# Encoder layer on one core: pooling's and the attention's projections as pairs, the middle's stages in another order, tiles kept in DRAM between their making and their use

## The chip, the cores and the metric

The kernel runs on one core of one Trainium2 chip, as one program and one launch. The metric is the device time of that core in microseconds; the time before is 2240.25 us, the median of three runs (2239.61 to 2243.97). A core has five engines, each with its own queue of instructions that it takes in order: TensorE (PE in the profile) multiplies, VectorE (DVE) and ScalarE (ACT) do elementwise work, GpSimd (POOL) and SyncE (SP) here only issue DMAs. Work on two engines overlaps unless one waits for the other's result, or for a place in memory.

## The reference

One layer of a bidirectional encoder over 256 tokens of width 2048, in float32:

```
x = x + 0.5 * swiglu(rmsnorm(x, ffn1_norm), ffn1_w_gate, ffn1_w_up, ffn1_w_down)
h = rmsnorm(x, mix_norm)
proj = h @ w_in       # u_pool 1024 | q 1536 | k 1536 | v 1536 | q_mem 1024 | gates 3 x 2048
y_pool = pooling_branch(u_pool, pool_w, pool_scale) @ w_up_pool
y_attn = dilated_attention_branch(q, k, v, positions) @ w_up_attn      # 3 groups of 4 heads, rotary q and k
y_mem  = memory_branch(q_mem, rmsnorm(mem, mem_norm), w_mem_kv) @ w_up_mem      # 4 heads, 256 memory tokens
merged = gates_0 * y_pool + gates_1 * y_attn + gates_2 * y_mem
x = x + merged @ w_out
x = x + 0.5 * swiglu(rmsnorm(x, ffn2_norm), ffn2_w_gate, ffn2_w_up, ffn2_w_down)
return rmsnorm(x, final_norm)
```

## The kernel before

**Products.** Every float32 factor is split into a high part (float32r, made by ACT, `wh`) and the rest (made by DVE, `wl`), and a product is three matmuls: low times high, high times high, high times low. A step of PE is one such matmul, 128x128 times 128x512. A plain product of the 256 tokens with 512 columns of a weight (`gemm`) takes, for 2048 rows of the weight, 16 row blocks x 2 token halves x 3 = 96 matmuls into two PSUM banks called `acc`. Its weights come as four tiles `wf` of 128x2048 (1 MB each), loaded by SP; each needs one `wh` on ACT and one `wl` on DVE.

**Pairs.** `pair_gemm` makes two such products at once, 1024 columns, in eight steps over pairs of row blocks, into eight banks called `q1` to `q8`. A step with eight products costs 24 matmuls, as much as in two plain products. A step out of the tuple `sevens` takes seven products, 21 matmuls, by a scheme of sums of blocks; it costs DVE more: `sums` of weight blocks (one add of 128x1024, two of 128x512), their split (`sumsh` on ACT in two pieces, `sumsl` on DVE), and a split of three blocks instead of four (128x1536). The left operand must have sums too; `lhs_mix` has them for steps 0, 2, 3 and 5 (`SEVEN_MIX`). When a bank's last product is done, `finish` brings it to SBUF, with four subtractions and four additions on DVE and one copy on ACT where sevens are used.

**The middle.** Between the two SwiGLU blocks stand, in this order: keys, values and query of the memory branch, twice (`mem_head` makes the four heads beside them); two plain products for pooling (u, with `pooling` beside what follows); for each of three head groups g the plain products Q, K, V, and, ahead of groups 1 and 2, the pooling gates of two chunks as a pair (`gated_pair(0, 0)`, `gated_pair(0, 2)`) with their two products with `w_up_pool`; the memory gates 0 and 1 as plain products with the attention's scores beside them (`attend`); the memory gates 2 and 3 as a pair; the attention gates as two pairs with three sevens each; four products with `w_out`. `PAIRED` says which gates are pairs and with which sevens.

After Q or K, `rotate` turns the columns by the rotary tables on DVE, and `turn_pieces` transposes the result: two DVE transposes of 32x32 squares into a spare tile, then 16 ACT copies of 32x256 (`qkT<-swap`).

**Places.** Large tiles share a ring of 23 slots. Held for long before are `lhs_mix` (6 slots), the memory's and pooling's left operands (`mem_lhs`, `pool_lhs`, 2 each), one `qkT` for each head group, and two tiles for the three V and the mask (`v01`, `v2`). One step of a pair with sevens uses 6 slots while it runs (`wf`, `wh`, `wl`, `sums`, `sumsh`, `sumsl`). Four tiles `tmp` and two `half` serve the rest.

**What sets the order.** The source only records instructions (`Plan.record`); `Plan.issue` then plays them through with costs of its own, gives out places, and writes each engine's order. Pieces of side work stand in a list (`later`, filled by `queue`) and are taken out between the row blocks of a product (`pop`). DMAs of SP and of POOL go out in the order of recording. All instructions have the line of the call in `Plan.issue`, L240, so the profile is read by tile names.

Of the kernel before, what the change touches and what calls it, by code (L numbers as in the profile page):

```python
# [9 lines left out]
F32 = mybir.dt.float32  # L10
# [417 lines left out]
def tile_encoder_layer(ctx: ExitStack, tc: tile.TileContext, a: dict, out: bass.AP):  # L428
# [816 lines left out]


    w_in = a["w_in"]
    mem_lhs = [lslot() for _ in range(2)]
    THREE = ((1, 0), (0, 0), (0, 1))

    def mem_head(qT, kT, v, h, L):
# [53 lines left out]
        return [scores], [*turns, parts], [lambda: values(0), lambda: values(1), lambda L=L: result(L)]  # L1305

    rope_work = rope_pieces()
    for n in range(2):
        queue(rope_work.pop(0))
        acc = gemm(mem_lhs_in, a["w_mem_kv"], 0, n * CW)  # L1310
        s = tmp([P, T, CW], "km")
        scaled_copy(s, acc, mem_rstd[0])
        kT = transposed(s)
        acc = gemm(mem_lhs_in, a["w_mem_kv"], 0, MEMW + n * CW)
        v = slot([P, 2, T, CW], F32R, "vm")
        scaled_split(v, acc, mem_rstd[0])
        queue(rope_work.pop(0))
        acc = gemm(lhs_mix, w_in, 0, C_M + n * CW)
        s = tmp([P, T, CW], "qm")
        scaled_copy(s, acc, rstd2)  # L1320
        qT = transposed(s)
        pending.add(id(mem_lhs[n]))
        (s0, t0, v0), (s1, t1, v1) = [mem_head(qT, kT, v, h, mem_lhs[n]) for h in range(2)]
# [4 lines left out]
        queue(lambda n=n: pending.discard(id(mem_lhs[n])))  # L1328


    band = slot([P, 4, T, S], F32R, "band")
# [51 lines left out]
    for n in range(2):  # L1383
        pending.add(id(pool_lhs[n]))
        queue(rope_work.pop(0))
        acc = gemm(lhs_mix, w_in, 0, n * CW)
        u = slot([P, 2, T, CW], F32R, "u")
        scaled_split(u, acc, rstd2)
        queue(lambda n=n, u=u: pooling(n, u))
        queue(lambda n=n: pending.discard(id(pool_lhs[n])))  # L1390


    MD = [dr.tile([P, T, CW], F32, name=f"merged{n}") for n in range(NCH)]
# [81 lines left out]
    qkT = [slot([P, 2, HEADS, S], F32, "qkT") for _ in GROUPS]  # L1475
    v01 = slot([P, 2, T, CW], F32, "v01")
    v2 = slot([P, 2, T, CW], F32, "v2")
    values = [v01[:, 0], v01[:, 1], v2[:, 0]]
    mask = v2[:, 1]
    nc.gpsimd.dma_start(out=mask, in_=a["mask"])  # L1480

    for g in range(3):
        if g:
            all_gated(0, (2 * g - 2, 2 * g - 1), pool_lhs, a["w_up_pool"])
        for sel, c0 in enumerate((C_Q, C_K)):
            acc = gemm(lhs_mix, w_in, 0, c0 + g * CW)
            r = tmp([P, T, CW], "rot")
            s = tmp([P, T, CW], "swap")

            def rotate(t, acc=acc, r=r, s=s):  # L1490
                src = acc[t].rearrange("p (h d) -> p h d", h=HEADS)
# [3 lines left out]
                nc.vector.tensor_mul(rt, src, cos.unsqueeze(1).to_broadcast([P, HEADS, P]))  # L1495
# [3 lines left out]
                nc.vector.tensor_mul(  # L1499
                    st[:, :, H:], src[:, :, :H], sin[:, H:].unsqueeze(1).to_broadcast([P, HEADS, H])  # L1500
                )
                nc.vector.tensor_add(r[:, t], r[:, t], s[:, t])

            queue(*(lambda t=t, f=rotate: f(t) for t in range(T)), soon=True)
            queue(*turn_pieces(qkT[g][:, sel], r, s))
        acc = gemm(lhs_mix, w_in, 0, C_V + g * CW)
        scaled_copy(values[g], acc, rstd2)

    attn_lhs = [lslot()]

# [1 line left out]
    def scores(h, state):  # L1512
        p = tmp([P, T, 2 * S], "p")
        for t in range(T):
            b = bank([P, 2 * S])
            blk = slice(t * P, (t + 1) * P)
            nc.tensor.matmul(b[:, :S], qkT[0][:, 0, h, blk], qkT[0][:, 1, h], start=True, stop=True)
            for g in (1, 2):
                c = S + (g - 1) * P
                nc.tensor.matmul(  # L1520
                    b[:, c : c + P], qkT[g][:, 0, h, blk], qkT[g][:, 1, h, blk], start=True, stop=True
                )
            nc.vector.tensor_add(p[:, t], b, mask[:, t])
# [12 lines left out]

    def turned_scores(state):
        def piece(i):
            if i == 0:
                state["pT"] = blocks_of(state["p"])  # L1540
                state["turns"] = turn_pieces(state["pT"], state["p"], tmp([P, T, 2 * S], "squares"))
            state["turns"][i]()

        return [lambda i=i: piece(i) for i in range(6)]
# [17 lines left out]
    def attend(n):  # L1562

        mine = [heads.pop(0) for _ in range(HEADS // len(alone))]
        states = [{} for _ in mine]
        for h, state in zip(mine, states):
            queue(lambda h=h, state=state: scores(h, state))
            queue(*[lambda: None] * (5 // len(mine)))
# [13 lines left out]
    all_gated(  # L1582
        1, range(NCH), attn_lhs, a["w_up_attn"], done=lambda n: merged_lhs.append(transposed(merged[n], shift=MERGED_MOVED))
    )


    lhs3 = pair_tiles(SEVEN)
# [150 lines left out]
```

## Time and profile before

| | |
|---|---|
| Runs | 2239.61, 2243.97, 2240.25 us; median 2240.25 |
| Profiled execution | 2241.2 us, of which 2239.5 us from the first to the last instruction |
| Granted TensorE clock | 0.998 of full speed |
| VectorE, ScalarE busy | 1892.4 us (85%), 1630.1 us (73%) |
| POOL | 264 instructions, 199.8 us |
| DMA | 531.36 MB, 237 GB/s on the mean |

The page cuts the span in 40 slices; the middle lies in slices 13 to 28 (696 to 1551 us). There DVE is busy 5 to 9 tenths and ACT 4 to 7, while in most slices of the two SwiGLU blocks DVE stands at 9 tenths or more. The profile calls PE busy throughout; since the end of a matmul is modelled, the rate is read from the distance of starts, that is, from the length of an unbroken run of matmuls divided by their count.

### The profile page before, as it was taken

Reading aid. Unit: us, or ns where it says so; the run is one execution under the profiler, and the core shown is the slowest. Engines: PE = TensorE matmul, PEld = TensorE weight load, DVE = VectorE, ACT = ScalarE, POOL = GpSimd, SP = SyncE. Lnnn points to the kernel's source line nnn. Section 1 sums busy time; section 2 is a strip of 40 time slices with the busy share of each in tenths; the row PEclk is TensorE's granted clock in tenths of the full one; section 3 lists DMA queues with packets and bytes.
Section 4 is the critical chain, followed back from the end, with each engine's and each line's share of the span. In section 5 each row is a group of like instructions: output and inputs, shape, how many; then the busy total and the mean of one; then the engine's idle time right before and its main releaser. Section 6 shows DMA issues by size and latency. Waiting matters only on the chain.

```text
span 2239.5 us, 26840 instructions
## 1 busy us (share of the span) xinstructions
PE 2223.7 (99%) x9906; PEld 1838.4 (82%) x9906; DVE 1892.4 (85%) x1738; ACT 1630.1 (73%) x2101; POOL 199.8 (9%) x264
## 2 busy tenths in 40 slices
PE   9999999999999999999999999999999999999998
PEld 7888888888887888888788888878888888888887
DVE  7999999999986865785776688977999999999995
ACT  8877777877777687654546774779777777777773
POOL 0011111111120000000000000000011111111110
PEclk9999999999999999999999999999999999999999
DMA  9688898988995564565464577666589989888892
GB/s 376 213 249 248 257 273 259 258 251 259 274 320 202 185 229 151 179 223 217 169 256 172 176 241 266 253 211 212 186 226 264 255 249 270 254 250 254 260 340 105
DMA packets 128995, 531.36 MB, mean 237 GB/s; under 512 B 15072, under 2 KB 15328, under 8 KB 102752
## 3 DMA queue, kind: packets, MB, share of 16 engines
q1 hardware_dynamic: 94608, 444.15, 55.7%
q0 software_dynamic: 33824, 84.95, 18.6%
q8 instruction: 77, 1.26, 0.2%
q10 hardware_dynamic: 432, 0.56, 0.1%
q14 instruction: 54, 0.44, 0.1%
HBM read 460.40 MB, written 50.33 MB: 228 GB/s over the span
## 4 chain that ended last, share of the span: by engine, by line
PE 95%; DMA 1%; DVE 1%; issue 1%; ACT 1%; POOL 0%; SPq 0%; DVEq 0%; POOLq 0%; ACTq 0%
PE q L240 48%; PE acc L240 29%; PE down L240 18%; PE bank L240 2%; DVE wl L240 1%; DMA wf<-in_ffn_w_up 1%; DMA xt<-in_memT 1%; ACT wh L240 0%; DMA wf<-in_w_in 0%; DVE up L240 0%; SPq L240 0%; POOL xs L240 0%; DVE squares L240 0%; POOL x L240 0%; DVE xs L240 0%
## 5 line engine op out<-in xcount | busy, mean ns | idle before, releaser
L240 DVE TENSOR_TENSOR wl<-wf,wh 128x2048 fp32r<-128x2048 f32 (+2 forms) x422 | 876.2, 2085 | 114.6 <-ACT wh L240 112.7
L240 ACT ACTIVATE wh<-wf 128x2048 fp32r<-128x2048 f32 (+2 forms) x422 | 732.1, 1750 | 127.2 <-DMA wf<-in_w_in 68.1
L240 PE MATMUL acc<-wh,lhs 128*128 128x512 f32 x1568 | 485.7, 391 | 0.0
L240 PE MATMUL down<-wh,lhs 128*128 128x512 f32 x1152 | 356.4, 391 | 0.0
L240 ACT ACTIVATE sumsh<-sums 128x1024 fp32r<-128x1024 f32 x266 | 280.9, 1060 | 98.0 <-DVE sums L240 95.8
L240 PE MATMUL q<-wh,seven 128*128 128x512 f32 x1102 | 342.9, 389 | 0.0
L240 PEld LDWEIGHTS acc<-wh,lhs 128*128 128x128 f32 x1568 | 293.4, 188 | 60.1
L240 DVE TENSOR_TENSOR sumsl<-sums,sumsh 128x2048 fp32r<-128x2048 f32 x133 | 303.5, 2282 | 46.1 <-ACT sumsh L240 43.9
L240 PE MATMUL q<-sumsh,seven 128*128 128x512 f32 x1064 | 321.3, 389 | 0.0
L240 PE MATMUL q<-wh,lhs 128*128 128x512 f32 x1024 | 310.4, 390 | 2.1 <-ACT wh L240 2.1
L240 PE MATMUL acc<-wl,lhs 128*128 128x512 f32 x784 | 305.7, 390 | 1.6 <-DVE wl L240 1.6
L240 PEld LDWEIGHTS down<-wh,lhs 128*128 128x128 f32 x1152 | 215.1, 188 | 47.7 <-ACT y L240 3.6
L240 PEld LDWEIGHTS q<-wh,seven 128*128 128x128 f32 x1102 | 206.8, 188 | 43.1
L240 PEld LDWEIGHTS q<-sumsh,seven 128*128 128x128 f32 x1064 | 199.6, 188 | 41.4
L240 PEld LDWEIGHTS q<-wh,lhs 128*128 128x128 f32 x1024 | 192.4, 188 | 43.6 <-ACT wh L240 3.3
L240 PE MATMUL down<-wl,lhs 128*128 128x512 f32 x576 | 224.2, 389 | 0.0
L240 PE MATMUL q<-wl,seven 128*128 128x512 f32 x551 | 213.5, 389 | 0.2 <-DVE wl L240 0.2
L240 POOL DMA_DIRECT2D x<-y x144 | 123.9, 860 | 811.3 <-ACT y L240 779.5
L240 ACT ACTIVATE y<-down 128x512 f32<-128x512 f32 x144 | 86.0, 597 | 148.2 <-PE down L240 118.6
L240 DVE TENSOR_TENSOR sums<-sums,wf 128x512 f32<-128x512 f32 x266 | 184.1, 692 | 9.0
L240 PE MATMUL q<-wl,lhs 128*128 128x512 f32 x512 | 190.6, 389 | 0.2 <-DVE wl L240 0.2
L240 PE MATMUL q<-sumsl,seven 128*128 128x512 f32 x532 | 185.1, 389 | 0.0
(184 smaller groups left out, 2287.4 us busy)
## 6 DMA issues: line engine op xcount, KB each, us to landing
wf<-in_ffn_w_down SPq DMA_DIRECT2D x88, 1024.0 KB, 7.6
wf<-in_ffn_w_gate SPq DMA_DIRECT2D x174, 512.0 KB, 5.9
wf<-in_ffn_w_up SPq DMA_DIRECT2D x174, 512.0 KB, 7.1
wf<-in_w_in SPq DMA_DIRECT2D x60, 1024.0 KB, 4.9
wf<-in_w_in SPq DMA_DIRECT2D x80, 512.0 KB, 5.1
x<-y POOLq DMA_DIRECT2D x144, 256.0 KB, 6.9
wf<-in_w_mem_kv SPq DMA_DIRECT2D x16, 1024.0 KB, 5.2
wf<-in_w_out SPq DMA_DIRECT2D x16, 1024.0 KB, 5.4
```

Source lines behind the costliest of these rows:

```text
L240: return getattr(getattr(self.nc, engine), name)(*map(real, args), **{k: real(v) for k, v in kw.items()})
```

## The change

- Pooling's two plain products become one pair with four sevens (`POOLED`, `make_pooled`).
- Q and K of group 1 become a pair with four sevens, those of group 2 a pair with three (`ROTATED`, `make_turned`); group 0 stays plain. A paired Q and K is rotated from the SBUF tiles `gate` and `up`, where the cosine product now stands behind the two sine products.
- The attention gates of chunks 0 and 1 get four sevens instead of three.
- The stages stand in a list, `STAGES`: Q and K of group 0, pooling's pair, V0, the pooling gates 0 and 1, the pair Q and K of group 1, V1, the pooling gates 2 and 3, the pair of group 2, V2.
- Tiles wait in DRAM: each memory head is copied to SBUF and written out (`MD_MEM`), and read back and split late (`recalled_heads`); Q and K of groups 0 and 1 are written out head by head (`keep`, `QKD`) and read back for two heads at a time (`recall_two`, 1 MB each); V0 and V1 are written out and read back with the mask (`recall`).
- The fourth chunk of `merged` is transposed by PE (`MERGED_PE`, eight matmuls with the identity) instead of by DVE and ACT. The ACT copies that turn the attention's probabilities are put 80 places later in the order (`SCORED`). The rotary tables are made a little earlier.

```diff
-    (0, 0): (0, 2, 3, 5), (0, 2): (0, 2, 3, 5), (2, 2): (0, 2, 3, 5), (1, 0): (2, 3, 5), (1, 2): (2, 3, 5),
+    (0, 0): (0, 2, 3, 5), (0, 2): (0, 2, 3, 5), (2, 2): (0, 2, 3, 5), (1, 0): (0, 2, 3, 5), (1, 2): (2, 3, 5),
 }
+ROTATED = {1: (0, 2, 3, 5), 2: (2, 3, 5)}
+SCORED = 80
+POOLED = (0,2,3,5)
+STAGES = [
+    ("turned", 0), ("pool", 0), ("values", 0), ("gates", 0), ("turned", 1), ("values", 1), ("gates", 2), ("turned", 2), ("values", 2),
+]
+MERGED_PE = (3,)
...
-        def result(L):
-            j = 2 * h
-            split(L[:, 0, j : j + 2], L[:, 1, j : j + 2], state["b"])
+        def result():
+            y = half_tmp([P, 2, S], F32, "head")
+            nc.scalar.activation(y, state["b"], AF.Copy)
+            nc.gpsimd.dma_start(out=kept, in_=y)
...
+    def make_pooled():
...
+        if POOLED:
+            flush()
+            pair_gemm(lhs_mix, (w_in, w_in), (0, CW), range(KB // 2), POOLED, out, soon=True)
...
+    def make_values(g):
+        acc = gemm(lhs_mix, w_in, 0, C_V + g * CW)
+        if g == 2:
+            scaled_copy(values[2], acc, rstd2)
+            return
+        v = tmp([P, T, CW], "v")
+        scaled_copy(v, acc, rstd2)
+        queue(lambda: nc.gpsimd.dma_start(out=VD[g], in_=v))
...
+        def part(n, half):
+            if not half:
+                held[n] = tmp([P, 4, S], "heads")
+                for k in range(2):
+                    nc.gpsimd.dma_start(out=held[n][:, 2 * k : 2 * k + 2], in_=MD_MEM[2 * n + k])
+                mem_lhs[n:] = [lslot()]
+            else:
+                split(mem_lhs[n][:, 0], mem_lhs[n][:, 1], held[n])
...
+    def recall_two(i):
+        both = slot([P, 2, 2, 2, S], F32, "qk")
+        nc.gpsimd.dma_start(out=both, in_=QKD[i])
...
+        if g in ROTATED:
+            cols = (C_Q + g * CW, C_K + g * CW)
+            pair_gemm(lhs_mix, (w_in, w_in), cols, range(KB // 2), ROTATED[g], out_qk, soon=True)
...
+        def keep(g=g, qkT=qkT):
+            for h in range(HEADS):
+                nc.gpsimd.dma_start(out=QKD[h // 2][:, h % 2, :, g], in_=qkT[:, :, h])
+
+        if g < 2:
+            queue(keep)
+        else:
+            last_group = qkT
+            queue(*recalled_heads(), lambda: recall_two(0))
+            recall()
...
+    def turn_merged(n):
+        if n not in MERGED_PE:
+            merged_lhs.append(transposed(merged[n], shift=MERGED_MOVED))
+            return
+        L, pieces = turned_lhs(merged[n], (4, 5, 6, 7))
+        merged_lhs.append(L)
+        queue(*pieces, soon=True)
```

How this moves instructions is shown at three places. The first is PE where pooling's projection begins. Before, it is a plain product into two `acc` banks, three matmuls for each token half and row block:

```order
L240 MATMUL acc_6763<-wh_6679,seven_5373 128x512 x2
L240 MATMUL acc_6763<-wl_6700,seven_5373 128x512
L240 MATMUL acc_6770<-wh_6679,seven_5373 128x512 x2
L240 MATMUL acc_6770<-wl_6700,seven_5373 128x512
L240 MATMUL acc_6763<-wh_6679,seven_5373 128x512 x2
```

Now it stands behind the last matmuls of K of group 0 and is a pair, whose products of sums read `sumsh` and `sumsl`:

```order
L247 MATMUL acc_6978<-wl_6915,lhs_5782 128x512
L247 MATMUL q_7209<-sumsh_7076,seven_5373 128x512 x2
L247 MATMUL q_7209<-sumsl_7118,seven_5373 128x512
L247 MATMUL q_7215<-sumsh_7076,seven_5373 128x512 x2
L247 MATMUL q_7220<-wh_7095,seven_5373 128x512 x2
L247 MATMUL q_7220<-wl_7136,seven_5373 128x512
```

Over the whole program PE has 36 matmuls of 128x512 fewer and eight transposes of 128x128 more; DVE has 68 instructions more, ACT 13 more, POOL 22 DMAs more, and SP loads `w_in` 128 times in halves (512 KB) and 36 times in whole tiles instead of 80 and 60 times.

The second place is ACT where Q and K of group 2 are turned (`qkT<-swap`, behind the third pair and beside V2). Before, weight tiles are split between the two runs of 16 copies:

```order
L240 ACTIVATE wh_9195<-wf_9155 128x2048
L240 ACTIVATE qkT_9206<-swap_9158 32x2x4x32 x16
L240 ACTIVATE wh_9258<-wf_9211 128x2048
L240 ACTIVATE wh_9272<-wf_9236 128x2048
L240 ACTIVATE wh_9322<-wf_9285 128x2048
L240 ACTIVATE wh_9346<-wf_9306 128x2048
L240 ACTIVATE qkT_9206<-swap_9309 32x2x4x32 x16
```

Now the two runs stand close together, with the first split of recalled memory heads (`lhs<-heads`) between them and the second behind V2's copy, all ahead of the next weight tile:

```order
L247 ACTIVATE wh_9475<-wf_9438 128x2048
L247 ACTIVATE qkT_9492<-swap_9446 32x2x4x32 x16
L247 ACTIVATE lhs_9548<-heads_9487 128x1024
L247 ACTIVATE qkT_9492<-swap_9484 32x2x4x32 x16
L247 ACTIVATE v_9273<-acc_9436,rstd_5808 128x512
L247 ACTIVATE lhs_9626<-heads_9550 128x1024
L247 ACTIVATE wh_9632<-wf_9554 128x2048
```

The third place is POOL's queue of DMAs around the same time (`bg` is the gates' bias, `merged` the sum of the branches in DRAM, `v` the tiles of V and the mask, `qk` the recalled Q and K of two heads). Before, the bias for the memory gates follows right behind the merge of the pooling gates:

```order
L240 DMA merged_8964<-gate_8782 128x1024
L240 DMA merged_9030<-up_8825 128x1024
L240 DMA bg_9038<-in_b_gate 128x512
L240 DMA bg_9044<-in_b_gate 128x512
L240 DMA merged_8103<-gate_9634 128x1024
```

Now nine other reads stand around the first bias, the large ones of Q and K last, behind the memory heads:

```order
L247 DMA merged_9167<-up_8943 128x1024
L247 DMA v_9273<-in_mask 128x1024
L247 DMA v_9294<-values_7815 128x1024
L247 DMA v_9294<-values_8739 128x1024
L247 DMA bg_9311<-in_b_gate 128x512
L247 DMA heads_9487<-heads_6550 128x512
L247 DMA heads_9487<-heads_6589 128x512
L247 DMA heads_9550<-heads_7132 128x512
L247 DMA heads_9550<-heads_7167 128x512
L247 DMA qk_9568<-qk_7321 128x2048
L247 DMA qk_9581<-qk_7332 128x2048
L247 DMA bg_9589<-in_b_gate 128x512
```

What moved: the reads of the memory heads wait for a free `tmp`, and whatever holds them up holds up the reads of Q and K behind them, which the attention's first scores on PE need.

More of the change, by code (lines that the diff above doesn't have):

```diff
@@ L1247, in tile_encoder_layer, with mem_head @@
     w_in = a["w_in"]
-    mem_lhs = [lslot() for _ in range(2)]
+    MD_MEM = [dr.tile([P, 2, S], F32, name=f"heads{h}") for h in range(4)]
+    mem_lhs = []
     THREE = ((1, 0), (0, 0), (0, 1))
-    def mem_head(qT, kT, v, h, L):
+    def mem_head(qT, kT, v, h, kept):
         state = {}
@@ L1298, in values @@
                     )
-        def result(L):
-            j = 2 * h
-            split(L[:, 0, j : j + 2], L[:, 1, j : j + 2], state["b"])
+        def result():
+            y = half_tmp([P, 2, S], F32, "head")
+            nc.scalar.activation(y, state["b"], AF.Copy)
+            nc.gpsimd.dma_start(out=kept, in_=y)
         turns = [lambda i=i: turn(i) for i in range(6)]
-        return [scores], [*turns, parts], [lambda: values(0), lambda: values(1), lambda L=L: result(L)]
+        return [scores], [*turns, parts], [lambda: values(0), lambda: values(1), result]
     rope_work = rope_pieces()
@@ L1317, in tile_encoder_layer @@
         queue(rope_work.pop(0))
+        if n:
+            queue(*rope_work)
         acc = gemm(lhs_mix, w_in, 0, C_M + n * CW)
@@ L1321, in tile_encoder_layer @@
         qT = transposed(s)
-        pending.add(id(mem_lhs[n]))
-        (s0, t0, v0), (s1, t1, v1) = [mem_head(qT, kT, v, h, mem_lhs[n]) for h in range(2)]
+        (s0, t0, v0), (s1, t1, v1) = [mem_head(qT, kT, v, h, MD_MEM[2 * n + h]) for h in range(2)]
         wait = [lambda: None]
@@ L1381, in pooling @@
                 split(L[:, 0, j], L[:, 1, j], b[:, db], s)
[L1383 to L1390, printed above, removed]
+    def make_pooled():
+        for n in range(2):
+            pending.add(id(pool_lhs[n]))
+        out, us = [], []
+        if POOLED:
+            flush()
+            pair_gemm(lhs_mix, (w_in, w_in), (0, CW), range(KB // 2), POOLED, out, soon=True)
+        for n in range(2):
+            acc = [out[n][:, t] for t in range(T)] if out else gemm(lhs_mix, w_in, 0, n * CW)
+            us.append(slot([P, 2, T, CW], F32R, "u"))
+            scaled_split(us[n], acc, rstd2)
+            for k in (0, 1) if out and n else () if out else (n,):
+                queue(lambda k=k: pooling(k, us[k]))
+                queue(lambda k=k: pending.discard(id(pool_lhs[k])))
     MD = [dr.tile([P, T, CW], F32, name=f"merged{n}") for n in range(NCH)]
@@ L1474, in tile_encoder_layer @@
     queue(scale_rope)
[L1475 to L1484, printed above, removed]
-        for sel, c0 in enumerate((C_Q, C_K)):
[L1486 to L1491, printed above, removed]
+    QKD = [dr.tile([P, 2, 2, 2, S], F32, name=f"qk{i}") for i in range(HEADS // 2)]
@@ new lines, in tile_encoder_layer, with recall @@
+    VD = [dr.tile([P, T, CW], F32, name=f"values{g}") for g in range(2)]
+    def make_values(g):
[6 more added lines that the diff above has]
+        queue(lambda: nc.gpsimd.dma_start(out=VD[g], in_=v))
+    qk_of = {}
+    values = []
+    def recall():
+        v01 = slot([P, 2, T, CW], F32, "v01")
+        v2 = slot([P, 2, T, CW], F32, "v2")
+        values.extend([v01[:, 0], v01[:, 1], v2[:, 0], v2[:, 1]])
+        nc.gpsimd.dma_start(out=values[3], in_=a["mask"])
+        for g in range(2):
+            nc.gpsimd.dma_start(out=values[g], in_=VD[g])
@@ new lines, in recalled_heads @@
+    def recalled_heads():
+        held = {}
+        def part(n, half):
[6 more added lines that the diff above has]
+                split(mem_lhs[n][:, 0], mem_lhs[n][:, 1], held[n])
+        return [lambda n=n, half=half: part(n, half) for n in range(2) for half in range(2)]
@@ new lines, in recall_two, with make_turned, rotate @@
+    def recall_two(i):
+        both = slot([P, 2, 2, 2, S], F32, "qk")
+        nc.gpsimd.dma_start(out=both, in_=QKD[i])
+        for h in range(2):
+            qk_of[2 * i + h] = [both[:, h, :, 0], both[:, h, :, 1], last_group[:, :, 2 * i + h]]
+    def make_turned(g):
+        nonlocal last_group
+        qkT = slot([P, 2, HEADS, S], F32, "qkT")
+        out_qk = []
+        if g in ROTATED:
+            cols = (C_Q + g * CW, C_K + g * CW)
+            pair_gemm(lhs_mix, (w_in, w_in), cols, range(KB // 2), ROTATED[g], out_qk, soon=True)
+        for sel, c0 in enumerate((C_Q, C_K)):
+            acc = None if out_qk else gemm(lhs_mix, w_in, 0, c0 + g * CW)
+            r = out_qk[sel] if out_qk else tmp([P, T, CW], "rot")
+            squares = []
+            def rotate(t, acc=acc, r=r, squares=squares):
+                if not squares:
+                    squares.append(tmp([P, T, CW], "swap"))
+                s = squares[0]
+                src = (acc[t] if acc else r[:, t]).rearrange("p (h d) -> p h d", h=HEADS)
@@ L1501, in rotate, with turns @@
                 )
+                nc.vector.tensor_mul(rt, src, cos.unsqueeze(1).to_broadcast([P, HEADS, P]))
                 nc.vector.tensor_add(r[:, t], r[:, t], s[:, t])
+            def turns(i, r=r, squares=squares, state={}, key=(g, sel), qkT=qkT):
+                if i == 0:
+                    state[key] = turn_pieces(qkT[:, key[1]], r, squares[0])
+                state[key][i]()
             queue(*(lambda t=t, f=rotate: f(t) for t in range(T)), soon=True)
-            queue(*turn_pieces(qkT[g][:, sel], r, s))
-        acc = gemm(lhs_mix, w_in, 0, C_V + g * CW)
-        scaled_copy(values[g], acc, rstd2)
+            queue(*(lambda i=i, f=turns: f(i) for i in range(6)))
+        def keep(g=g, qkT=qkT):
[7 more added lines that the diff above has]
+            recall()
+    last_group = None
+    for step, n in STAGES:
+        if step == "pool":
+            make_pooled()
+        elif step == "turned":
+            make_turned(n)
+        elif step == "values":
+            make_values(n)
+        else:
+            all_gated(0, (n, n + 1), pool_lhs, a["w_up_pool"])
     attn_lhs = [lslot()]
@@ L1516, in scores @@
             blk = slice(t * P, (t + 1) * P)
-            nc.tensor.matmul(b[:, :S], qkT[0][:, 0, h, blk], qkT[0][:, 1, h], start=True, stop=True)
+            qk = qk_of[h]
+            nc.tensor.matmul(b[:, :S], qk[0][:, 0, blk], qk[0][:, 1], start=True, stop=True)
             for g in (1, 2):
@@ L1520, in scores @@
                 nc.tensor.matmul(
-                    b[:, c : c + P], qkT[g][:, 0, h, blk], qkT[g][:, 1, h, blk], start=True, stop=True
+                    b[:, c : c + P], qk[g][:, 0, blk], qk[g][:, 1, blk], start=True, stop=True
                 )
-            nc.vector.tensor_add(p[:, t], b, mask[:, t])
+            nc.vector.tensor_add(p[:, t], b, values[3][:, t])
         mx, den = small([P, T]), small([P, T])
@@ L1540, in piece @@
                 state["pT"] = blocks_of(state["p"])
-                state["turns"] = turn_pieces(state["pT"], state["p"], tmp([P, T, 2 * S], "squares"))
+                state["turns"] = turn_pieces(state["pT"], state["p"], tmp([P, T, 2 * S], "squares"), SCORED)
             state["turns"][i]()
@@ L1565, in attend @@
         states = [{} for _ in mine]
+        if n == 0:
+            queue(lambda: recall_two(1))
         for h, state in zip(mine, states):
@@ L1581, in tile_encoder_layer @@
     merged_lhs = []
-    all_gated(
-        1, range(NCH), attn_lhs, a["w_up_attn"], done=lambda n: merged_lhs.append(transposed(merged[n], shift=MERGED_MOVED))
-    )
+    def turn_merged(n):
[5 more added lines that the diff above has]
+        queue(*pieces, soon=True)
+    all_gated(1, range(NCH), attn_lhs, a["w_up_attn"], done=turn_merged)
     lhs3 = pair_tiles(SEVEN)
```

2 lines of the change are left out of this document (removed).

## The prediction

> **What bounds the kernel now.** I read the page's first and fourth part, then the chain of waits in order of time, then who waited for whom on PE.
>
> ```profile
> span 2239.5 us, 26840 instructions
> PE 2223.7 (99%) x9906; PEld 1838.4 (82%) x9906; DVE 1892.4 (85%) x1738; ACT 1630.1 (73%) x2101; POOL 199.8 (9%) x264
> PE 95%; DMA 1%; DVE 1%; issue 1%; ACT 1%; POOL 0%; SPq 0%; DVEq 0%; POOLq 0%; ACTq 0%
> ```
>
> PE makes 95% of the chain that ended last. Since ends of matmuls are modelled, its rate is read from unbroken pieces of that chain (start, length, what, count), one at the end of the middle and one in the second SwiGLU:
>
> ```profile
> 1551.54 86.36 PE q L240 x381
> 1870.72 12.24 PE q L240 x54
> ```
>
> 86.36 / 381 and 12.24 / 54 both give 0.2267 us for one matmul of 128x512, in two very different stages: that is PE's full rate here. What it loses beside that from 30 us on to the end is four waits, the whole answer of the trace for PE:
>
> ```profile
> PE bank L240 <- DVE xs L240: 2.1, 2, 1.7
> PE q L240 <- ACT wh L240: 2.1, 1, 2.1
> PE acc L240 <- DVE wl L240: 1.6, 1, 1.6
> PE q L240 <- DVE wl L240: 0.2, 1, 0.2
> ```
>
> Six microseconds in 2200. So the time is PE's count of matmuls times 0.2267 us, and a change gains what it takes off the count, as long as the other engines keep up.
>
> [...]
>
> **How near the other engines are.** The columns are stretch, its length, then busy time and count of PE, PEld, DVE, ACT and POOL, the clock, DMA share and GB/s. The rows are the pair of pooling gates 0 and 1 before, the two products behind it, and one period of the second SwiGLU:
>
> ```profile
> 956.80:997.50 40.70, 40.70 (x181) 33.73 (x180) 35.95 (x29) 25.20 (x20) 0.00 (x0) 1.00 0.67 233
> 997.50:1019.30 21.80, 21.80 (x98) 18.06 (x97) 15.19 (x12) 11.04 (x8) 0.55 (x1) 1.00 0.61 218
> 1870.70:1932.00 61.30, 61.30 (x272) 50.59 (x271) 58.16 (x47) 47.96 (x57) 8.62 (x10) 1.00 0.89 257
> ```
>
> In the SwiGLU DVE works 58.16 of 61.30 us (95%) and PE loses nothing. The middle is far below that, so there is room for the dearer products with sums.
>
> **The change part by part.** *Matmuls.* Each step with seven products saves 3 matmuls. New are 4 (pooling), 4 (Q and K of group 1), 3 (group 2) and 1 (attention gates 0 and 1): 12 steps, 36 matmuls, 36 x 0.2267 = **-8.2 us**. Added are eight transposes by PE. The nearest row:
>
> ```profile
> L240 PE MATMUL bank<-ident,up 128*128 128x128 f32 x16 | 2.4, 272 | 0.0
> ```
>
> 2.4 / 16 = 0.15 us each, **+1.2 us**.
>
> *DVE.* Durations of the forms in the middle (busy, mean ns):
>
> ```profile
> L240 DVE TENSOR_TENSOR wl<-wf,wh 128x2048 fp32r<-128x2048 f32 x112 | 253.8, 2283 | 89.6 <-ACT wh L240 87.8 <-PE acc L240 1.5
> L240 DVE TENSOR_TENSOR sumsl<-sums,sumsh 128x2048 fp32r<-128x2048 f32 x18 | 41.2, 2287 | 8.1 <-ACT sumsh L240 5.9 <-PE q L240 2.1
> L240 DVE TENSOR_TENSOR wl<-wf,wh 128x1536 fp32r<-128x1536 f32 x18 | 31.5, 1751 | 0.0
> L240 DVE TENSOR_TENSOR sums<-sums,wf 128x512 f32<-128x512 f32 x36 | 24.9, 692 | 1.2
> L240 DVE TENSOR_TENSOR sums<-wf 128x1024 f32<-128x1024 f32 x18 | 21.8, 1214 | 1.6 <-DMA wf<-in_w_in 1.6
> L240 DVE TENSOR_TENSOR swap<-acc,rope 128x256 f32<-128x256 f32 x24 | 8.9, 413 | 0.0
> L240 DVE TENSOR_TENSOR rot<-rot,swap 128x512 f32<-128x512 f32 x12 | 8.3, 692 | 0.4
> L240 DVE TENSOR_TENSOR rot<-acc,rope 128x512 f32<-128x512 f32 x12 | 8.2, 686 | 12.8 <-PE acc L240 12.8
> L240 DVE STREAM_TRANSPOSE swap<-rot 128x512 f32<-128x512 f32 x12 | 7.8, 690 | 0.2
> L240 DVE TENSOR_TENSOR gate<-q,gate 128x512 f32<-128x512 f32 x10 | 6.9, 690 | 4.1 <-PE q L240 4.1
> ```
>
> A step with seven costs 1.21 + 2 x 0.69 + 2.29 + 1.75 = 6.64 us, one with eight 2.28. A pair with four sevens: 4 x 6.64 + 4 x 2.28 + 8 x 0.69 (`finish`) = 41.2 us, against 180 x 0.2267 = 40.8 us of PE. Alone it would just not fit; the single product behind each pair is what pays for it. The tightest is the pair Q and K of group 1 with V1: DVE 41.2, four splits 9.1, the rotation of both 4 x (2 x 0.41 + 0.69 + 0.69) = 8.8, four transposes 2.8, in all 61.9; PE 40.8 + 96 x 0.2267 = 62.6 us. That is 99%. The pair of gates with its two products comes to 41.2 + 9.1 and some 6 for gates and merges, 56 of 62.6. For group 2, with three sevens, it is 36.8 + 20.7 + 2.4 for the memory heads (two of 128x1024 at 1.21), 60 of 63.3.
>
> At 99% the price lies between nothing, if DVE with a backlog never idles, and what DVE idled in the SwiGLU row, 61.30 - 58.16 = 3.1 us, which makes 65.0 and overshoots PE by 2.4. I take **+2.4**, because a DVE at 95% is the nearest row there is.
>
> *The two waits that PE has in this region.* The first is of 2.1 + 0.2 us, inside the pair of pooling gates 2 and 3. SP's row and ACT's row (start, length; in brackets idle time and what ended it), then what held SP's loads around there:
>
> ```profile
> 1098.92 4.88 SPq L240 DMA_DIRECT2D wf<-in_w_in  x6
> 1104.69 1.91 ACT L240 ACTIVATE wh<-wf 128x2048 fp32r<-128x2048 f32 x1 [4.89 <-DMA wf<-in_w_in]
> ```
>
> ```profile
> SPq L240 <- PE q L240: 11.4, 3, 8.0
> ```
>
> SP waited up to 8.0 us for PE to give a slot back. Held at that place are 14 slots of 23: `lhs_mix` 6, `pool_lhs` 2, `mem_lhs` 2, `qkT` 2, `v01`, `v2`. Now it is 9 (6 + 2 + one `qkT`), since heads, Q, K and V lie in DRAM. Fourteen free slots instead of nine are more than two steps of a pair instead of one and a half. I count the wait as gone, **-2.3 us**; the other end is nothing gained.
>
> The second, 1.6 us, falls into the first products with `w_out`:
>
> ```profile
> 1468.21 3.84 ACT L240 ACTIVATE merged<-squares 32x256 f32<-32x256 f32 x9 [6.19 <-DVE squares L240]
> 1471.49 6.65 DVE L240 TENSOR_TENSOR wl<-wf,wh 128x2048 fp32r<-128x2048 f32 x3
> ```
>
> Nine turning copies, which waited for DVE, stood ahead of a weight split on ACT. Now half of these copies are gone, and those left stand behind that split: **-1.6 us**. The other end is the same wait again.
>
> *Recalled tiles.* Let T be the end of the pair Q and K of group 2.
>
> ```profile
> L240 ACT ACTIVATE qkT<-swap 32x256 f32<-32x256 f32 x96 | 39.9, 416 | 12.8 <-PE acc L240 7.1 <-DVE swap L240 4.7
> xs<-x POOLq DMA_DIRECT2D x24, 256.0 KB, 6.4
> mem<-in_mem POOLq DMA_DIRECT2D x2, 1024.0 KB, 13.3
> ```
>
> DVE finishes the rotation and squares of Q at about T + 6.5 (0.69 + 4.4 + 1.4) and those of K, one weight split between them, at T + 14.6. The first `heads` tile gets its place at T + 6.5 and lands 6.4 us plus one issue (0.9) later, at T + 14; ACT, done with its 16 copies (6.7 us) at T + 13.4, waits under 1 us; behind it stand the copies of K, V2's copy and the next weight tile's `wh`, which PE needs only 144 matmuls behind T, at T + 32.6. The read of Q and K goes out at about T + 16.4 and lands 13.3 us later, T + 30. The first scores stand 156 matmuls behind T in PE's order, T + 35.4. So the reads cost **nothing**, with 5 us to spare. V and the mask are asked for earlier and needed later. Writing the tiles out delays nobody; POOL is busy 9%.
>
> **The sum:** -8.2 + 1.2 + 2.4 - 2.3 - 1.6 = **-8.5 us**. The profiled execution took 2241.2 us, so it would be 2232.7; the median of the runs lies 0.95 below that execution, which gives **2231.8 us**.
>
> **The rivals.**
>
> *The recall comes late.* POOL takes its DMAs in order. If the second `heads` tile gets its place only when ACT has turned K (T + 22), the read of Q and K goes out at T + 24 and lands at T + 37, 2 us late; if it also waits for a slot as SP did (8.0 us), 10 us late. PE stands still at the scores. In the middle, 6 us: 2231.8 + 6 = 2238. For it speaks that four `tmp` places serve everything at this spot; against it, the 5 us to spare and the free slots. [...]
>
> *Nothing gained.* What PE saves becomes waits for operands of the same size: about 2240 us. For it: DVE's sum is 99% in one stretch; against it: 95% costs PE nothing in the SwiGLU.
>
> *Slower: DVE's idle time inside a pair stays.* In the row of the pair above DVE idled 40.7 - 35.95 = 4.75 us while PE was full. If it idles so in every pair with four sevens, each needs 41.2 + 4.75 = 45.9 us where PE has 40.8, and if the slots don't let the single product behind make up for it, PE loses 5.1 us in each of five pairs (pooling, gates 0 and 1, Q and K, gates 2 and 3, attention gates 0 and 1): 25.5 - 7.0 = +18.5, 2258 us. It ends slower by more than 0.2% from 2.3 us of idle per pair on ((7.0 + 4.5) / 5). Against it: the same pair ran before without loss, since part of its sums was made ahead and its additions behind.
>
> **How the numbers follow.** 0.2% is 4.5 us, about what a measurement of this kernel can tell from no change. The forecast has 0.75, the late recall 0.11, nothing gained 0.06, slower 0.08. Faster by over 0.2% means below 2235.8 us: 0.75. Within: 0.17. Slower: 0.08. The low end of the range is the forecast without the price for DVE, less 1 us for the spread of runs: 2228.4; the high end takes in the late recall and most of nothing gained: 2239.5.
>
> **What would show it.** Right: 36 matmuls fewer at 0.2267 us in the list of PE; the pairs of pooling and of Q and K in 41 us each; no wait of PE for `wh` in the pair of gates 2 and 3, nor for `wl` at `w_out`; PE's first `bank<-qk` behind the landing of `qk`. Wrong: PE waiting for `wl` or `sumsl` inside pairs with DVE near 100% (DVE bounds), or for `qk` or `heads` (late recall), or the two old waits in their old size.

## The result, and the profile after

The changed kernel takes **2228.66 us** (median of four runs, 2228.47 to 2228.84); the kernel before 2239.93 (median of four runs, the three above and one of 2239.24). The ratio is 0.9943, with a 95% interval of 0.9928 to 0.9958; the two medians alone give 0.9950. The forecast was 2231.8 from 2240.25, 8.5 us less; measured are 11.3 us less. The low end of the forecast's range, 2228.4, is 0.9947 of 2240.25, so the gain reaches that end or passes it. The direction and most terms hold, and the gain is larger than the sum made it.

The head of the page after, and its line on the chain that ended last:

```profile
span 2226.8 us, 26976 instructions
PE 2214.1 (99%) x9878; PEld 1830.7 (82%) x9878; DVE 1955.7 (88%) x1806; ACT 1644.8 (74%) x2114; POOL 212.9 (10%) x286
PE 93%; issue 5%; DMA 1%; DVE 0%; ACT 0%; POOL 0%; SPq 0%; DVEq 0%; POOLq 0%; ACTq 0%
```

PE has 28 instructions fewer (36 matmuls less, 8 transposes more). DVE works 63.3 us longer and POOL 13.1, and neither shows up on the chain. From 30 us on, this is the whole answer of the trace after for what PE waited for (total, times, longest):

```profile
PE bank L247 <- DVE xs L247: 1.2, 1, 1.2
PE down L247 <- ACT y L247: 0.6, 1, 0.6
```

Both lie outside the middle. The two old waits that the prediction named, 2.1 + 0.2 us for `wh` and `wl` in a pair and 1.6 us for `wl` at the first products with `w_out`, are gone, and nothing has taken their place.

**A measure for the middle.** Spans differ from run to run by a few microseconds, and most of that lies ahead of the middle: the memory branch's keys start on PE between 692.59 and 701.53 us in the profiled executions below. So I measure the middle by itself, from the start of the keys' first group of matmuls to the start of the last matmul with `w_out`. In the timeline of PE (start, length, what) these two stand for the kernel before at

```profile
696.00 0.62 PE L240 MATMUL acc<-wh,lhs 128*128 128x512 f32 x2
...
1551.15 0.39 PE L240 MATMUL acc<-wl,lhs 128*128 128x512 f32 x1
```

and for the kernel after at

```profile
694.12 0.62 PE L247 MATMUL acc<-wh,lhs 128*128 128x512 f32 x2
...
1537.17 0.39 PE L247 MATMUL acc<-wl,lhs 128*128 128x512 f32 x1
```

That is 855.15 us before and 843.05 after: **12.1 us less**. A second profiled execution of the changed kernel gave 843.04, so this measure repeats to far below a microsecond where the span doesn't. The windows view gives the engines' work in these two stretches (length, then busy time and count of PE, PEld, DVE, ACT, POOL, the clock, DMA share, GB/s). Before:

```profile
695.95:1551.30 855.35, 851.42 (x3867) 708.68 (x3867) 629.47 (x645) 573.29 (x789) 23.37 (x40) 1.00 0.59 208
```

After:

```profile
694.10:1537.30 843.20, 843.20 (x3839) 702.80 (x3838) 693.83 (x714) 588.16 (x802) 36.54 (x62) 1.00 0.63 221
```

PE's busy time now equals the stretch, 843.20 of 843.20, where 3.93 us were idle before. DVE took on 64.4 us and went from 74% (629.47 / 855.35) to 82%.

**The pairs.** Pieces of the chain in order of time, after (start, length, what, count): pair Q and K of group 1, V1, pair of pooling gates 2 and 3, their two products, pair of group 2.

```profile
1014.87 40.80 PE q L247 x180
1055.66 21.76 PE acc L247 x96
1077.42 40.80 PE q L247 x180
1118.22 21.76 PE acc L247 x96
1139.98 41.48 PE q L247 x183
...
1539.12 80.28 issue
```

40.80 / 180 and 21.76 / 96 are both 0.2267 us, PE's full rate, through five stages without a gap. The last row, in the second SwiGLU, is most of the 5% issue on the page; PE was busy in all of it (the last row of the next fence), the chain merely names no releaser. What DVE did (windows, after: the products with `w_up_pool` ahead of the pair Q and K of group 1, that pair, V1, pair and V1 together, and at last that piece of the SwiGLU):

```profile
992.90:1014.70 21.80, 21.80 (x97) 18.03 (x97) 21.11 (x19) 12.09 (x11) 0.54 (x1) 1.00 0.43 141
1014.70:1055.50 40.80, 40.80 (x181) 33.80 (x180) 32.18 (x26) 20.81 (x14) 0.53 (x1) 1.00 0.76 270
1055.50:1077.30 21.80, 21.80 (x98) 18.06 (x97) 21.15 (x28) 15.16 (x34) 0.53 (x1) 1.00 0.37 121
1014.70:1077.30 62.60, 62.60 (x278) 51.85 (x277) 53.33 (x54) 35.97 (x48) 1.06 (x2) 1.00 0.62 218
...
1539.10:1619.40 80.30, 80.30 (x356) 66.52 (x355) 71.19 (x65) 61.88 (x78) 0.02 (x1) 1.00 0.51 174
```

The pair that was to need 41.2 us of DVE shows 32.18, and pair and V1 together 53.33 where the prediction had 61.9. The rest is done by neighbours: in the same two products before (the row at 997.50 in the prediction) DVE worked 15.19 us, now 21.11, since sums for the pair are made there in advance.

**The recall.** The tile views after give, for the reads of the memory heads, their first use by ACT, the reads of Q and K, and PE's use of those (mean duration in ns as least, median and greatest; first and last start in us):

```profile
L247 POOL DMA_DIRECT2D heads<-heads x4: 537/537/542, 1188.1 to 1195.5; - x4
L247 ACT ACTIVATE lhs<-heads x2: 1047/1056/1065, 1194.8 to 1203.2; 128x1024 fp32r<-128x1024 f32 x2
L247 POOL DMA_DIRECT2D qk<-qk x2: 534/534/534, 1196.2 to 1196.7; - x2
DMA to landing us min/median/max: 2.5/5.8/11.4
L247 PE MATMUL bank<-qk x32: 272/326/382, 1216.7 to 1255.7; 128*128 128x256 f32 x16, 128*128 128x128 f32 x16
```

With T = 1181.3 (end of the pair of group 2) the first read goes out at T + 6.8, ACT splits at T + 13.5, Q and K are asked for at T + 15, land within 11.4 us, by T + 27, and PE takes them up at T + 35.4 without a wait. The forecast had T + 6.5, 14, 16.4, 30 and 35.4.

### The profile page after: what moved, and what is told of

The parts are those of the page before. It is cut to its first block, busy times and chain, and to the rows that moved or that the text cites. A ratio compares the mean times of both kernels' runs of the same rounds, so it can differ in the third digit from the quotient of the medians.

```text
span 2226.8 us, 26976 instructions
## 1 busy us (share of the span) xinstructions
PE 2214.1 (99%) x9878; PEld 1830.7 (82%) x9878; DVE 1955.7 (88%) x1806; ACT 1644.8 (74%) x2114; POOL 212.9 (10%) x286
## 4 chain that ended last, share of the span: by engine, by line
PE 93%; issue 5%; DMA 1%; DVE 0%; ACT 0%; POOL 0%; SPq 0%; DVEq 0%; POOLq 0%; ACTq 0%
PE q L247 50%; PE acc L247 24%; PE down L247 18%; PE bank L247 2%; DMA wf<-in_ffn_w_up 1%; DMA xt<-in_memT 0%; DMA late_gate<-gate 0%; DVE up L247 0%; DVE wl L247 0%; SPq L247 0%; POOL xs L247 0%; ACT wh L247 0%; POOL x L247 0%; DVE xs L247 0%; ACT L247 0%
## 5 line engine op out<-in xcount | busy, mean ns | idle before, releaser
L247 PE MATMUL acc<-wh,lhs 128*128 128x512 f32 x1376 | 425.2, 390 | 0.0
L247 ACT ACTIVATE sumsh<-sums 128x1024 fp32r<-128x1024 f32 x290 | 305.4, 1059 | 117.4 <-DVE sums L247 107.6
L247 PE MATMUL q<-wh,lhs 128*128 128x512 f32 x1216 | 372.2, 389 | 1.1 <-ACT wh L247 1.1
L247 DVE TENSOR_TENSOR sumsl<-sums,sumsh 128x2048 fp32r<-128x2048 f32 x145 | 330.8, 2282 | 46.0 <-ACT sumsh L247 43.2
L247 PE MATMUL q<-wh,seven 128*128 128x512 f32 x1174 | 364.6, 389 | 0.0
L247 PE MATMUL q<-sumsh,seven 128*128 128x512 f32 x1160 | 352.4, 389 | 0.0
L247 PEld LDWEIGHTS acc<-wh,lhs 128*128 128x128 f32 x1376 | 256.6, 188 | 52.3
L247 PEld LDWEIGHTS q<-wh,lhs 128*128 128x128 f32 x1216 | 228.0, 188 | 49.5 <-ACT wh L247 2.2
L247 PE MATMUL acc<-wl,lhs 128*128 128x512 f32 x688 | 267.4, 389 | 0.0
L247 PE MATMUL q<-wl,lhs 128*128 128x512 f32 x608 | 231.4, 389 | 0.1
```

Of the source, the lines that this page charges most:

```text
L247: return getattr(getattr(self.nc, engine), name)(*map(real, args), **{k: real(v) for k, v in kw.items()})
```

## The experiments

Three questions were open: whether the count of matmuls is paid in full, why DVE's 99% cost nothing, and what took the two old waits away. Each kernel is the changed one with one edit, if not said otherwise. "Middle" is the measure above, read from one profiled execution of each kernel; times are medians of five to eleven runs, and ratios are to runs of the kernel before that were taken beside them.

**The change once more.**

> The changed kernel once more, beside fresh runs of the one before. If the difference is what the trace adds up to (36 matmuls x 0.2267 = 8.2 us less, eight transposes 0.9 more, the two waits of PE in the middle, 2.3 and 1.6, gone), the medians lie 11.2 us apart. If part of the 12.7 us between the two profiled spans was also gained in every run (the wait at the memory branch's start, 2.1 against 1.2 us, and small slips), 12 to 13 apart.

2229.33 us, ratio 0.9949 (0.9937 to 0.9962); middle 843.04. The two measurements of the change agree within their intervals. The medians lie 11.8 us apart, between the two values expected, so this run does not decide between them.

**The change without its new sevens.**

```diff
-(1, 0): (0, 2, 3, 5)
+(1, 0): (2, 3, 5)
-ROTATED = {1: (0, 2, 3, 5), 2: (2, 3, 5)}
+ROTATED = {}
-POOLED = (0,2,3,5)
+POOLED = ()
```

> The change without its 12 new steps of seven products: pooling and Q, K of all groups as plain products, attention gates 0 and 1 with three sevens, but the new order of stages, the tiles in DRAM and the transposes by PE kept. Theory (what the sevens take off PE's count is paid in full, the rest is the two waits): 8.2 us slower than the changed kernel, about 3 us faster than before. Rival (the order and the free slots are what gains, and the sums cost DVE what they save PE): within 2 us of the changed kernel.

2236.96 us, ratio 0.9983 (0.9974 to 0.9992); middle 851.16, **8.11 more** than with them, where 36 x 0.2267 = 8.16. The medians of the two lie 7.6 us apart. So the sevens pay their count in full, and DVE's extra work costs nothing beside it. The rest of the change (order, DRAM, transposes) is worth 855.15 - 851.16 = 4.0 us.

**`merged` turned by DVE and ACT again.**

```diff
-MERGED_PE = (3,)
+MERGED_PE = ()
```

> The changed kernel with the fourth chunk of merged turned by VectorE and ScalarE as before (16 copies more on ScalarE, eight transposes fewer on PE). Theory (PE's wait of 1.6 us in the products with w_out came from these copies ahead of a weight split): the wait is back, less 0.9 us for the transposes: 0.7 us slower than the changed kernel. Rival (the wait went with something else): 0.9 us faster than the changed kernel and no wait at w_out.

2231.61 us, ratio 0.9957 (0.9945 to 0.9969), not to be told from the change; middle 843.98, 0.93 more. The wait at `w_out` is back, in PE's list of waits of this kernel:

```profile
PE acc L247 <- DVE wl L247: 1.6, 1, 1.6
```

From start to start it cost PE 1.79 us more than a matmul. Less the eight transposes, which start 0.11 us apart in the chain after (0.66 us for six of them, 0.87 for eight), that is +0.92. Both terms of this part are shown: the transposes take 0.9 us and remove a wait of 1.8.

**The kernel before, with the fourth chunk of `merged` turned by PE.**

```diff
+MERGED_PE = (3,)
...
-    all_gated(1, range(NCH), attn_lhs, a["w_up_attn"], done=lambda n: merged_lhs.append(transposed(merged[n], shift=MERGED_MOVED)))
+    all_gated(1, range(NCH), attn_lhs, a["w_up_attn"], done=turn_merged)
```

> The kernel before with one part of the change alone: the fourth chunk of merged transposed by PE. Theory (that part removes the wait of 1.6 us at w_out and costs 0.9): 0.7 us faster than before, PE's wait for wl at w_out gone, the one of 2.1 us in the pair of gates 2 and 3 still there. Rival (the wait went with the change's order): 0.9 us slower than before.

2241.35 us, ratio 0.9995 (0.9987 to 1.0004); middle 854.19, 0.96 less than before. Of this kernel's waits two answer to the old ones:

```profile
PE q L241 <- ACT wh L241: 2.1, 1, 2.1
...
PE q L241 <- DVE wl L241: 0.2, 1, 0.2
```

The wait at `w_out` is gone here too and the one in the pair stays. The turning by PE alone removes the former, and has nothing to do with the latter.

**More work for DVE in the stretch forecast at 99%.** Useless additions are queued at the start of V1 and taken out beside it: a memset and two additions, or a memset and six.

```diff
+    def ballast(n):
+        x = slot([P, 4, CW], F32, "ballast")
+        nc.vector.memset(x, 0.0)
+        def one():
+            nc.vector.tensor_add(x, x, x)
+        queue(*([one] * n))
...
     def make_values(g):
+        if g == 1:
+            ballast(2)          # 6 in the second kernel
```

> The changed kernel with useless work on VectorE in V1's stage, behind the pair Q and K of group 1: one fill of 128x2048 and two additions of 128x2048 (2.29 us each), some 6 us. The prediction's sum (VectorE at 61.9 of 62.6 us in this stretch, what does not fit stops PE): 5 us slower than the changed kernel. The trace of the change (53.3 of 62.6 us busy, since work slides to the stretches beside it): no slower.

> The same with six additions, some 15 us. The prediction's sum: 14 us slower than the changed kernel. The trace's room of 9.3 us in this stretch: up to 6 us slower, less if the next stretch (4.9 us of room) takes some of it. If VectorE's room is shared over the whole middle: under 1 us.

With two: 2228.47 us, ratio 0.9944 (0.9931 to 0.9958); middle 843.06, **unchanged**. (The profiled execution is the slowest of the five, 2236.33 us; its middle starts late, at 701.53.) The groups of this kernel (busy, mean ns; idle before) show the work that was added, 6.3 us:

```profile
L247 DVE TENSOR_TENSOR ballast<-ballast 128x2048 f32<-128x2048 f32 x2 | 4.5, 2265 | 0.0
L247 DVE MEMSET ballast<- 128x2048 f32 x1 | 1.8, 1765 | 0.4 <-DVE wl L247 0.4
```

If DVE had been 99% full or 2.4 us over, these 6.3 us would have come out on PE. They didn't. Nor did idle time in the stretch take all of them. In this kernel's windows for the same stretch and for the pair of gates 2 and 3 behind it

```profile
1022.10:1084.70 62.60, 62.60 (x278) 51.84 (x277) 55.40 (x54) 35.40 (x46) 1.07 (x2) 1.00 0.64 219
1084.70:1125.50 40.80, 40.80 (x182) 33.80 (x181) 39.03 (x32) 29.36 (x26) 3.41 (x5) 1.00 0.83 296
```

DVE has 2.1 us more in each than after (53.33, and 36.92 from 1077.3 to 1118.1 us). The other 2 us lie behind these two: the work slid on into the next stages.

With six (15.5 us): 2238.35 us, ratio 0.9986 (0.9978 to 0.9995); middle 851.80, 8.75 more. PE waits here for sums inside the pair of gates 2 and 3:

```profile
PE q L247 <- ACT sumsh L247: 5.4, 2, 4.6
```

None of the three amounts expected (14, up to 6, under 1) fits. This looks like the overshoot that was forecast, yet in this kernel's windows (pair Q and K of group 1 with V1) DVE still idles 7.2 us of 62.6:

```profile
1015.40:1078.00 62.60, 62.60 (x278) 51.83 (x277) 55.43 (x53) 35.14 (x45) 1.07 (x2) 1.00 0.63 218
```

What decided is where the additions stood. DVE's timeline at the end of V1:

```profile
1076.49 1.22 DVE L247 TENSOR_TENSOR sums<-wf 128x1024 f32<-128x1024 f32 x1
1077.62 6.94 DVE L247 TENSOR_TENSOR ballast<-ballast 128x2048 f32<-128x2048 f32 x3
1084.48 1.41 DVE L247 TENSOR_TENSOR sums<-sums,wf 128x512 f32<-128x512 f32 x2
```

Three of them, 6.94 us, stand between the first and the second addition of the next pair's first sums, and `sumsh` and PE wait for these. The slack of the whole stretch can't be spent at that point.

**Slots held back.** Five slots (as many as the change gives back by DRAM) are kept occupied from ahead of `STAGES` to the attention's left operands, then two; then five in the kernel without new sevens.

```diff
+    held_back = [slot([P, 4, CW], F32, "held") for _ in range(5)]     # 2 in the second kernel
+    for h in held_back:
+        nc.gpsimd.memset(h[:, 0, :32], 0.0)
     for step, n in STAGES:
...
+    for h in held_back:
+        nc.gpsimd.memset(h[:, 0, :32], 0.0)
     attn_lhs = [lslot()]
```

> The changed kernel with five more slots of the ring held from the first stage of the list to the last, so that about as many are free as before. Theory (the wait of 2.3 us inside the pair of pooling gates 2 and 3 went because slots came free): a wait of PE for wh or wl of 1 to 4 us comes back in one of the pairs, and ScalarE waits for weights nearer to 58 us than to 13 in the stretch; 2230 to 2233. Rival (it went because the stages stand in another order): no wait in the pairs, 2228.7 as with the change.

> The changed kernel with two slots of the ring held through the list of stages instead of five. Theory (loads run ahead by whole steps of a pair, six slots each, and 14 free slots are two steps and two more): with 12 left two steps still fit, little is lost, under 3 us in the middle. Rival (each slot counts alike): 2/5 of the 13 us that five slots cost, about 5 us.

> The new order and the tiles in DRAM without the 12 new sevens (plain products, as in e1), and five slots held. Theory (it is the pairs with sums that need the slots): the loss is far below 13 us, about the 2.7 us that the kernel before lost in its pair of gates 2 and 3; middle 852 to 855. Rival (any stage needs them): 13 us over e1's 851.2.

| Kernel | Middle, us | us | Ratio to before |
|---|---|---|---|
| the change, five held | 856.01 (+13.0) | 2243.23 | 1.0012 (1.0003 to 1.0021) |
| the change, two held | 846.67 (+3.6) | 2233.9 | 0.9963 (0.995 to 0.9975) |
| no new sevens, five held | 851.77 (+0.6 on 851.16) | 2239.95 | 0.9989 (0.998 to 0.9998) |

With five held the change is worth nothing any more, and more is lost than either expectation had; with two held, 3.6 lies between "under 3" and "about 5". PE's loss is made of small waits, of which these rows belong to the pairs and to products (five held):

```profile
PE acc L247 <- DVE wl L247: 2.4, 3, 1.6
PE q L247 <- DVE sumsl L247: 1.6, 3, 0.9
PE q L247 <- ACT wh L247: 1.4, 3, 0.6
PE q L247 <- ACT v L247: 1.1, 1, 1.1
PE q L247 <- ACT sumsh L247: 1.0, 3, 0.6
```

The loss isn't spread evenly. By the starts of PE, pooling's pair takes 46.57 us instead of 40.82 and the pair of gates 2 and 3 takes 44.63 instead of 40.80; the pair of gates 0 and 1 and both pairs Q and K lose under 0.1 us each, and the other 3.4 us fall on products between and behind the pairs. With two held it is the same two pairs, 2.6 and 0.9 us. They are the two in which ACT turns a group's Q and K just ahead or inside (`qkT<-swap`, 874.7 to 893.3 and 1071.0 to 1087.8 us with five held). That these copies are the reason is likely but not tested. In the pair of gates 2 and 3 (1085.9 to 1130.6 us) PE waits for

```profile
PE q L247 <- ACT v L247: 1.1, 1, 1.1
PE q L247 <- ACT wh L247: 0.6, 1, 0.6
PE q L247 <- ACT sumsh L247: 0.6, 1, 0.6
PE q L247 <- DVE sumsl L247: 0.4, 1, 0.4
```

ACT's wait for tiles of `w_in` beside the stages, after,

```profile
ACT wh L247 <- DMA wf<-in_w_in: 13.2, 10, 2.8
```

becomes, with five held,

```profile
ACT wh L247 <- DMA wf<-in_w_in: 48.4, 21, 5.0
```

while it is just as long in the kernel without new sevens and with five held, and there costs 0.6 us:

```profile
ACT wh L247 <- DMA wf<-in_w_in: 60.8, 21, 6.0
```

This row is no measure of the scarcity: without new sevens and with nothing held it is 58.5 us too, and 58.0 before. What the runs show is that the same five slots cost 0.6 us without the new sevens and 13.0 with them.

They also answer a reason of the prediction, in two halves. With five held and no new sevens as few slots are free as before, and the pair of gates 2 and 3 takes 41.25 us, where it took 43.79 before; the one wait in the view from 30 us on, 0.6 us for `y`, lies outside the middle. So the new order of stages alone takes away most of the old wait, without free slots; which part of the order, no run here separates. In the changed kernel, however, this very pair loses 3.8 us as soon as five slots are held. With the new sevens around it, it stays free of waits only because slots are free.

**More sevens than the change has.** Two more (attention gates 2 and 3, and Q and K of group 2); one more (group 2 alone); and six more, where group 0 becomes a pair as well and all side work still queued is issued ahead of it.

```diff
-(1, 2): (2, 3, 5)
+(1, 2): (0, 2, 3, 5)             # not in the kernel with one more
-ROTATED = {1: (0, 2, 3, 5), 2: (2, 3, 5)}
+ROTATED = {1: (0, 2, 3, 5), 2: (0, 2, 3, 5)}     # with six more: 0: (0, 2, 3, 5) too
...
+        if g == 0:               # with six more only
+            flush()
```

> The change carried further: Q and K of group 0 as a pair with four sevens too, group 2 and the attention gates 2 and 3 with four instead of three: 6 steps of seven more, 18 matmuls fewer. Theory (PE's count sets the time, VectorE has room): 18 x 0.2267 = 4.1 us faster than the changed kernel, 2224.6. Rival (VectorE, which has about 12% of idle time left over the middle, becomes the bound where four pairs follow on one another): PE waits for wl or sumsl, no faster than the changed kernel.

> The changed kernel with four sevens instead of three for Q and K of group 2 and for the attention gates 2 and 3: 2 steps more, 6 matmuls fewer. Theory (PE's count is paid as long as no new wait comes): from the memory branch's start to the second SwiGLU 1.4 us less than the changed kernel's 843.05, no new wait of PE. Rival (VectorE bounds where a pair with four sevens is added): PE waits for wl or sumsl, 843 or more.

> The changed kernel with a fourth seven for Q and K of group 2 alone; the attention gates 2 and 3, where the run with two more sevens made PE wait, keep three. Theory (the wait there came from two pairs with four sevens so close together, with only 11 us of single products between; the pair of group 2 has V2 behind it): 3 matmuls fewer, 0.7 us off the middle (842.4 against 843.05), no wait of PE in the pairs. Rival (the wait at the attention gates comes from the changed order ahead of it): 843.5 or more.

| Sevens more | Matmuls | Middle, us | us | Ratio to before |
|---|---|---|---|---|
| 1 | -3 | 842.49 (-0.56; count alone -0.68) | 2229.64 | 0.9951 (0.9938 to 0.9965) |
| 2 | -6 | 845.16 (+2.1; count alone -1.36) | 2230.6 | 0.9949 (0.9937 to 0.9962) |
| 6 | -18 | 868.28 (+25.2; count alone -4.1) | 2254.47 | 1.0058 (1.0045 to 1.007) |

One more pays its count and has no wait in a pair: the shortest middle of all kernels here, though its time can't be told from the change's. With the second, in the attention gates 2 and 3, PE waits in that pair, and at `w_out`:

```profile
PE q L247 <- ACT sumsh L247: 0.9, 2, 0.6
PE q L247 <- ACT wh L247: 0.6, 1, 0.6
PE acc L247 <- DVE wl L247: 0.3, 1, 0.3
```

With six, the waits in the pair of group 0 and in pooling's pair behind it are large:

```profile
PE q L247 <- DVE sumsl L247: 7.1, 2, 6.3
PE bank L247 <- ACT pTs L247: 3.7, 2, 3.5
PE q L247 <- DVE wl L247: 3.3, 1, 3.3
```

That kernel doesn't tell whether the pair is to blame, or the memory branch's side work that was pushed ahead of it: the two edits were made together. It was a failed experiment in that respect. (The 12% of idle time in its expectation is DVE's over the whole execution; over the middle it is 18%.)

## Why the prediction was right in kind and short in size

| Term, us | Forecast | Measured | By |
|---|---|---|---|
| 36 matmuls fewer | -8.2 | -8.1 | the kernel without new sevens |
| eight transposes | +1.2 | +0.9 | starts 0.11 us apart |
| DVE overshoots in Q and K of group 1 with V1 | +2.4 | **0** | windows after; two additions more at no cost |
| wait in the pair of gates 2 and 3 | -2.3 | -2.6 | starts in the trace of before |
| wait at `w_out` | -1.6 | -1.8 | the kernel with `merged` by DVE and ACT |
| small gaps of before | 0 | -0.5 | rest |
| the middle | -8.5 | -12.1 | |

**The term that was mis-sized is DVE's, "+2.4".** The prediction charged all of the pair's 41.2 us, the splits of V1 and the rotation to one stretch of 62.6 us, got 61.9, and then took the price from the end where DVE's idle time in the SwiGLU adds to it. The step that failed was the closed stretch: DVE doesn't have to do a stage's work within the stage. Sums go ahead into the products of the stage before (21.11 us there where 15.19 were), and the stretch itself showed 53.33 us; 6.3 more were queued there for nothing, and two thirds of them came out in later stages. The price itself had no support in its row either: DVE idled 3.1 us there while PE lost nothing. The other end that was named, "nothing, if DVE with a backlog never idles", has the right value for another reason: DVE did idle, 9.3 us, and it cost nothing. The load of the whole middle, 82%, would have been the better measure for this term, though the six additions show that such a share doesn't rule out a loss at one place.

Of the other 1.2 us, 0.3 are the transposes, charged at the busy time of `bank<-ident,up` divided by its count (0.15 us) where their starts lie 0.11 apart; 0.5 are the two waits, taken from the list of waits instead of the distance of starts; the rest, small gaps, was not in the sum. The spans differ by 12.7 us, 0.6 more than the middles; that is inside what the part ahead of the middle varies by. The medians differ by 11.3 and, in the second measurement, 11.8.

**Right for the reason given.** PE is the bound and the count sets the time: 28 matmuls and transposes less in the list of PE, and 8.11 us for 36 x 0.2267. The wait at `w_out` went because of the turning by PE, as the kernel before with that one edit shows. The recall costs nothing, with landings 8 us ahead of PE's need where 5 were forecast. The trace has 7.1 and 11.4 us for the two reads of 1 MB, less than the 13.3 that the prediction used.

**Right for a reason that holds in part.** The wait in the pair of gates 2 and 3 is gone as forecast. That fourteen slots were free instead of nine is needed in the changed kernel (3.8 us lost there without five of them), but without the new sevens the new order removes most of the wait by itself. The free slots do more than the prediction asked of them: without five of them the middle is 13.0 us longer and the change ends at 1.0012 of before.

**The rivals.** "Slower" was right that pairs need slots. Its condition did not hold, since slots were free; with five held back, two of the five pairs that it names lose 5.8 and 3.8 us, and the middle 13.0 instead of its 25.5. That DVE's idle time inside the pairs causes this loss, as the rival had it, isn't shown. "Nothing gained" and "the recall comes late" have nothing in the traces for them.

## What to carry to other kernels

Where one engine has no gap, price a cut by its count at the rate of starts (here 36 x 0.2267 = 8.16 us, and 8.11 measured), and ask of the others whether the operands arrive in time, not whether a stage's work fits into the stage: DVE, off the bound here, spent the idle time of the stage ahead (21.11 us of work there where 15.19 were), and the middle took 13.0 us more when five slots fewer were free to work ahead in. Such buffers are the price of the cheaper product: free them first (here by parking long-lived tiles in DRAM), since two slots fewer took back 3.6 us and five took back all of it. And test a suspected limit by adding work to it: 6.3 us of ballast that cost nothing settled what a sum of durations had wrong.

## What the runs showed of the hardware

A wait of PE cost more than its length here. In the kernel with six additions PE waited 4.6 us, and the windows view of the stretch with this wait and what follows gives a granted clock of 0.93:

```profile
1078.00:1127.00 49.00, 43.60 (x179) 34.91 (x178) 46.87 (x35) 28.30 (x25) 3.41 (x5) 0.93 0.69 247
```

In the chain of waits the matmuls right behind it took twice their time, 5.06 us for 11 of them where 11 x 0.2267 = 2.5:

```profile
1087.03 5.06 PE q L247 x11
```

So of the 8.75 us lost some 3 are not the wait. The length of the wait alone doesn't decide this. In the profiled execution of the kernel before, PE waited twice for `xs` ahead of the middle, 2.1 us in all and at most 1.7, and a window right behind it has the granted clock at 0.50 (the column after POOL's):

```profile
686.30:689.70 3.40, 3.40 (x11) 2.61 (x10) 2.32 (x6) 3.40 (x7) 0.00 (x0) 0.50 0.22 84
```

The kernels with two additions and with two more sevens show such 3.4 us at 0.50 behind a wait of 2.5 or 2.6 us; over their whole profiled executions the mean clock is 0.998, and 0.999 after. Yet behind the wait of 2.1 us in the pair of gates 2 and 3 before, the window from 1104 to 1112 us has 1.00. What decides between these waits, no run here shows. The kernel with six more sevens has three such stretches, 23.8 us in all, and a mean clock of 0.994, so part of its 25.2 us is the clock's.

So the traces have matmuls at half rate behind some waits: 5.06 / 11 = 0.46 us each behind the one of 4.6 us, where they take 0.2267 us elsewhere, and a granted clock of 0.50 over 3.4 us behind the one of 1.7 us.
